# A low-rank update on one core: sixteen tokens a partition in each part, and two more engines' programs as loops

## The chip, the cores and the metric

The kernel runs on one core of one Trainium2 chip. The metric is device time in microseconds of one execution; the time before is the median of three runs. "Span" is the time between the first and the last instruction of one execution that was recorded by the hardware profiler. Engines are named as in the profile: PE is TensorE, DVE is VectorE, ACT is ScalarE, POOL is GpSimd and SP is SyncE.

## What is computed

```python
def setup_inputs():
    batch, seq, d_model, r = 16, 512, 768, 16
    # x [16, 512, 768], A [768, 16], B [16, 768], float32; scale 0.5

def reference(x, A, B, scale):
    lora = np.matmul(np.matmul(x, A), B)
    return (x + scale * lora).astype(np.float32)
```

There are 8192 tokens of 768 numbers. Each token is read once (25.2 MB), gets a rank-16 correction and is written once (25.2 MB).

## The kernel before

**Layout.** The 8192 tokens are 64 "token slots" of 128 partitions each; all of x stays on the chip in one tile, xs, of 64 slots x 768 float32 a partition. SyncE issues the transfers: eight loads of 2, 2, 4, 8, 8, 8, 16 and 16 slots, and ten stores of 2, 2, 4 and then 8 slots each (lists LOADS and STORES). Within a load of n slots a partition holds n consecutive tokens, so that its row is one contiguous run of n x 3 KB. All go through one queue, in the order of issue: loads 0 and 1, A, B, the other loads, then the stores. The last load goes over the place where A and B stood in float32, so SyncE waits for their conversion (prep) before it. Each store waits for a count of the semaphore added.

**Chunks.** Work goes by chunks of four slots, 16 in all. For each chunk:

- the four slots are narrowed to float16 in three tiles of 256 columns: xh0 and xh1 by VectorE, xh2 by ScalarE (function narrowed, L92 and L94). Each tile has one buffer;
- TensorE transposes them in six groups of four 128x128 matmuls with an identity (turned(0) to turned(5), L186), into three PSUM buffers; turned(0) and turned(1) read xh0, turned(2) and turned(3) xh1;
- ScalarE moves each group to the float16 tiles xt (L136);
- TensorE projects with A in six steps (projected(0) to projected(5), L194); ScalarE scales the result to yt (L140);
- TensorE multiplies with B, slot by slot (expanded(0) to expanded(3), L205), into two PSUM buffers lo_ps; VectorE adds each to xs in place (summed, L147) and posts freed.

**Order.** The engines are not tied by a scheduler; each has a program written out by hand, and semaphores between them. TensorE's program is a hardware loop over chunks; it consumes its semaphores one at a time (taken: wait for at least 1, then take 1 away). One pass is:

```python
for j in range(NX):            # NX = 3
    turned(j)
first()                        # both(0): expanded(0), expanded(1) of the chunk before
for j in range(NX, ND):        # ND = 6
    projected(j - NX)
    turned(j)
second()                       # both(2): expanded(2), expanded(3) of the chunk before
for j in range(NX, ND):
    projected(j)
```

Every expanded takes one freed, so that it waits for the sum two slots earlier. VectorE's and ScalarE's programs are written out for all 16 chunks and wait for absolute counts. VectorE does, in chunk c: refill xh0 for chunk c + 1 as soon as turned has counted turned(1) of chunk c, two sums of chunk c - 1, refill xh1 after turned(3), two more sums. A drain follows the last sum of each store, and posts added.

**Start.** VectorE narrows chunk 0, transposes A (L159), converts it to a_mm (L163) and B to b_mm (L165), and posts prep; TensorE's first projection waits for that.

Of the kernel before, what the change touches and what calls it, by code (L numbers as in the profile page):

```python
# [9 lines left out]
MM_DT = mybir.dt.float16  # L10


LOADS = [2, 2, 4, 8, 8, 8, 16, 16]
STORES = [2, 2, 4, 8, 8, 8, 8, 8, 8, 8]

CHUNK = 4

# [2 lines left out]
def kernel(  # L20
# [8 lines left out]
    nc = tc.nc  # L29
    fp32 = mybir.dt.float32  # L30
    add = mybir.AluOpType.add
    P = 128

    x2 = x.flatten_outer_dims()
    out2 = out.flatten_outer_dims()
    T, D = x2.shape
    R = A.shape[1]
    NT = T // P
    NC = NT // CHUNK
    ND = D // P  # L40
    NU = ND // 2
    NX = 3
    W = 2 * P
    NB = D // 32
# [4 lines left out]
    sb = ctx.enter_context(tc.tile_pool(name="sb", bufs=1))  # L49
    ps = ctx.enter_context(tc.tile_pool(name="ps", bufs=1, space=bass.MemoryType.PSUM))  # L50

    xs = sb.tile([P, NT, D], fp32, name="xs")
    ident = sb.tile([P, P], MM_DT, name="ident")
    a_mm = sb.tile([P, ND, R], MM_DT, name="a_mm")
    b_mm = sb.tile([R, D], MM_DT, name="b_mm")
    xh = [sb.tile([P, CHUNK, W], MM_DT, name=f"xh{u}") for u in range(NU)]
    xt = [sb.tile([P, CHUNK * P], MM_DT, name=f"xt{j}") for j in range(ND)]
    yt = sb.tile([R, CHUNK * P], MM_DT, name="yt")
    xt_ps = [ps.tile([P, CHUNK * P], fp32, name=f"xt_ps{b}") for b in range(NX)]
    yt_ps = ps.tile([R, CHUNK * P], fp32, name="yt_ps")  # L60
    lo_ps = [ps.tile([P, D], fp32, name=f"lo_ps{b}") for b in range(2)]
# [5 lines left out]
    b_f32 = xs[0:R, room + 2, :]  # L67

    def rows(t2, t0, n):
        return t2[ds(t0 * P, n * P), :].rearrange("(p s) d -> p s d", s=n)  # L70

    with tc.tile_critical():  # L72
        names = "zeroed ident a b a_t prep fed0 fed1 fed2 turned got proj y lora freed added".split()
        S = {k: nc.alloc_semaphore(name=f"s_{k}") for k in names}
        landed = [nc.alloc_semaphore(name=f"s_load{i}") for i in range(len(LOADS))]
        stored = nc.alloc_semaphore(name="s_stored")
        part_of = [i for i, n in enumerate(LOADS) for _ in range(n)]

        def load(i):
            t0, n = sum(LOADS[:i]), LOADS[i]  # L80
            nc.sync.dma_start(out=xs[:, t0 : t0 + n, :], in_=rows(x2, t0, n)).then_inc(landed[i], 16)

        known = set()

        def narrowed(engine, c, u):
            for i in sorted({part_of[c * CHUNK + s] for s in range(CHUNK)}):
                if (engine.engine, i) not in known:
                    known.add((engine.engine, i))
                    engine.wait_ge(landed[i], 16)
            src = xs[:, ds(c * CHUNK, CHUNK), ds(u * W, W)]  # L90
            if engine is nc.scalar:
                i = engine.copy(out=xh[u], in_=src)  # L92
            else:
                i = engine.tensor_copy(out=xh[u], in_=src)  # L94
            i.then_inc(S[f"fed{u}"], 1)


        nc.gpsimd.memset(a_rows, 0.0).then_inc(S["zeroed"], 1)  # L98
        nc.gpsimd.memset(ident, 0.0).then_inc(S["zeroed"], 1)  # L99
        nc.gpsimd.wait_ge(S["zeroed"], 2)  # L100
        nc.gpsimd.affine_select(  # L101
            out=ident, in_=ident, compare_op=mybir.AluOpType.not_equal, fill=1.0,
            base=0, pattern=[[-1, P]], channel_multiplier=1,
        ).then_inc(S["ident"], 1)


        load(0)
        load(1)
        nc.sync.wait_ge(S["zeroed"], 1)
        nc.sync.dma_start(  # L110
            out=a_rows[0:NB, :, :], in_=A.rearrange("(b a) r -> b a r", a=32)
        ).then_inc(S["a"], 16)
        nc.sync.dma_start(out=b_f32, in_=B).then_inc(S["b"], 16)
        for i in range(2, len(LOADS) - 1):
            load(i)
        nc.sync.wait_ge(S["prep"], 1)
        load(len(LOADS) - 1)
        done = 0
        for k, n in enumerate(STORES):
            i = part_of[done]  # L120
            t0, w = sum(LOADS[:i]), LOADS[i]
            nc.sync.wait_ge(S["added"], k + 1)
            piece = slice(done - t0, done - t0 + n)
            nc.sync.dma_start(
                out=rows(out2, t0, w)[:, piece, :], in_=xs[:, done : done + n, :]
            ).then_inc(stored, 16)
            done += n

        nc.gpsimd.wait_ge(stored, 16 * len(STORES))


        narrowed(nc.scalar, 0, 2)
        for c in range(NC):
            for j in range(ND):
                nc.scalar.wait_ge(S["turned"], ND * c + j + 1)
                nc.scalar.copy(out=xt[j], in_=xt_ps[j % NX]).then_inc(S["got"], 1)  # L136
            if c + 1 < NC:
                narrowed(nc.scalar, c + 1, 2)
            nc.scalar.wait_ge(S["proj"], c + 1)
            nc.scalar.activation(  # L140
                out=yt, in_=yt_ps, func=mybir.ActivationFunctionType.Copy, scale=sc
            ).then_inc(S["y"], 1)


        def summed(k):
            nc.vector.wait_ge(S["lora"], k + 1)
            nc.vector.tensor_tensor(  # L147
                out=xs[:, k, :], in0=xs[:, k, :], in1=lo_ps[k % 2], op=add
            ).then_inc(S["freed"], 1)
            if k + 1 in ends:  # L150
                nc.vector.drain().then_inc(S["added"], 1)  # L151

        ends = {sum(STORES[: i + 1]) for i in range(len(STORES))}
        nc.vector.sem_inc(S["freed"], 2)
        narrowed(nc.vector, 0, 0)
        narrowed(nc.vector, 0, 1)

        nc.vector.wait_ge(S["a"], 16)
        nc.vector.transpose(out=a_t, in_=a_rows.rearrange("b a r -> b r a")).then_inc(S["a_t"], 1)  # L159
        nc.vector.wait_ge(S["a_t"], 1)  # L160
        a_tv = a_t[:, :, 0:NB].rearrange("a r (c k) -> a k c r", k=4)
        for k in range(4):
            nc.vector.tensor_copy(out=a_mm[ds(32 * k, 32), :, :], in_=a_tv[:, k, :, :])  # L163
        nc.vector.wait_ge(S["b"], 16)
        nc.vector.tensor_copy(out=b_mm, in_=b_f32).then_inc(S["prep"], 1)  # L165
        for c in range(NC):
            for u in range(2):
                if c + 1 < NC:
                    nc.vector.wait_ge(S["turned"], ND * c + 2 * u + 2)
                    narrowed(nc.vector, c + 1, u)  # L170
                if c >= 1:
                    for s in range(2 * u, 2 * u + 2):
                        summed((c - 1) * CHUNK + s)
        for s in range(CHUNK):
            summed((NC - 1) * CHUNK + s)


        def taken(name):
            nc.tensor.wait_ge(S[name], 1).then_inc(S[name], -1)  # L179

        def turned(j):
            u, h = divmod(j, 2)
            if h == 0:
                taken(f"fed{u}")
            for s in range(CHUNK):
                i = nc.tensor.matmul(  # L186
                    xt_ps[j % NX][:, ds(s * P, P)], xh[u][:, s, ds(h * P, P)], ident,
                    start=True, stop=True,
                )
            i.then_inc(S["turned"], 1)  # L190

        def projected(j):
            taken("got")
            i = nc.tensor.matmul(  # L194
                yt_ps, a_mm[:, j, :], xt[j], start=(j == 0), stop=(j == ND - 1)
            )
            if j == ND - 1:
                i.then_inc(S["proj"], 1)

        def expanded(s):  # L200
            if s == 0:
                taken("y")
            taken("freed")
            for n0, w in n_splits:
                i = nc.tensor.matmul(  # L205
                    lo_ps[s % 2][:, ds(n0, w)], yt[:, ds(s * P, P)], b_mm[:, ds(n0, w)],
                    start=True, stop=True,
                )
            i.then_inc(S["lora"], 1)

        def chunk(first, second):
            for j in range(NX):
                turned(j)
            first()
# [3 lines that stand above are left out]
            second()  # L218
            for j in range(NX, ND):
                projected(j)  # L220

        def both(s):
            expanded(s)
            expanded(s + 1)

        nc.tensor.wait_ge(S["ident"], 1)
        chunk(lambda: nc.tensor.wait_ge(S["prep"], 1), lambda: None)
        with nc.Fori(1, NC, engines=(mybir.EngineType.PE,)):
            chunk(lambda: both(0), lambda: both(2))
        for s in range(CHUNK):  # L230
            expanded(s)
# [35 lines left out]
```

## Time and profile before

| | |
|---|---|
| median of three runs | 125.25 us (125.25 to 125.34) |
| the profiled execution | 125.31 us, span 123.5 us |
| busy: PE, DVE, ACT | 84.3, 80.2, 76.2 us |
| bytes, mean rate over the span | 50.45 MB, 408 GB/s |
| share of the span in which the queue's packets fill the 16 DMA engines | 96.4% |
| last sum of VectorE done, last store issued, last store landed | 101.1, 101.2, 122.5 us |

The page's second part cuts the span into 40 slices of 3.1 us; a digit is the busy share in tenths. A timeline line gives start, duration, engine, line, operation, output and inputs, how many in a row, and in brackets the idle time before it with what ended that. A line of windows gives a stretch, its length, the busy time of PE, PEld, DVE, ACT and POOL with numbers of instructions, the granted TensorE clock, the share of the DMA engines and GB/s.

### The profile page before, as it was taken

To read this page: it belongs to the slowest core of one execution; us is meant where nothing else is said; L and a number is where in the kernel's file an instruction comes from. 1 tells how busy PE (TensorE), PEld (TensorE's weight loads), DVE (VectorE), ACT (ScalarE), POOL (GpSimd) and SP (SyncE) were. 2 spreads that over 40 slices of the span, in tenths; PEclk is the share of its full clock that TensorE was granted. 3 is DMA by queue.
4 is the path that set the end of the run, shared out by engine and by line. 5 is a ranking of instruction groups with operands and counts; after the bars stand their busy time and mean duration, and the time that the engine had idled before them with its cause. 6 is when DMAs were issued, how large, how long until landed. Compare 5 with 4: busy or idle time off the path is not lost. (4 is left out here: it accounts for less than half of the span.)

```text
span 123.5 us, 1804 instructions
## 1 busy us (share of the span) xinstructions
PE 84.3 (68%) x608; PEld 39.7 (32%) x608; DVE 80.2 (65%) x102; ACT 76.2 (62%) x129; POOL 1.1 (1%) x7
## 2 busy tenths in 40 slices
PE   0024986999999999999999999999999420000000
PEld 0022342444445444454444544445444100000000
DVE  0049208888999999999899999999977770000000
ACT  0047598469889898898988989889896100000000
POOL 3000000000000000000000000000000000000000
PEclk9999999589999999999999999999999975555555
DMA  3999999999999699899889999999999999999990
GB/s 86 414 396 426 477 398 454 422 406 469 414 509 477 302 496 493 382 401 477 288 366 448 434 477 398 446 438 398 477 398 446 438 398 485 390 454 438 390 414 16
DMA packets 2662, 50.45 MB, mean 408 GB/s; under 512 B 316, under 2 KB 316, under 8 KB 868
## 3 DMA queue, kind: packets, MB, share of 16 engines
q1 hardware_dynamic: 2660, 50.43, 96.4%
q14 instruction: 2, 0.02, 0.0%
HBM read 25.26 MB, written 25.17 MB: 408 GB/s over the span
## 5 line engine op out<-in xcount | busy, mean ns | idle before, releaser
L147 DVE TENSOR_TENSOR xs<-xs,lo_ps 128x768 f32<-128x768 f32 x64 | 58.1, 950 | 5.5 <-PE lo_ps L205 4.8
L136 ACT CAST xt<-xt_ps 128x512 f16<-128x512 f32 x96 | 52.4, 577 | 10.1 <-PE xt_ps L186 8.4
L186 PE MATMUL xt_ps<-ident,xh 128*128 128x128 f16 x384 | 34.4, 229 | 8.6 <-PEq L179 8.6
L194 PE MATMUL yt_ps<-xt,a_mm 128*16 128x512 f16 x96 | 32.9, 396 | 1.8 <-PEq L179 1.6
L94 DVE CAST xh<-xs 128x1024 f16<-128x1024 f32 x32 | 22.0, 689 | 15.3 <-DMA xs<-in_x_dram 13.1
L186 PEld LDWEIGHTS xt_ps<-ident,xh 128*128 128x128 f16 x384 | 23.0, 102 | 26.9 <-issue 26.9
L205 PE MATMUL lo_ps<-b_mm,yt 16*128 16x512 f16 (+1 forms) x128 | 26.6, 324 | 5.4 <-PEq L179 3.5
L92 ACT CAST xh<-xs 128x1024 f16<-128x1024 f32 x16 | 16.8, 1048 | 0.0
L205 PEld LDWEIGHTS lo_ps<-b_mm,yt 16*128 16x128 f16 x128 | 9.6, 92 | 15.2 <-issue 9.5
L194 PEld LDWEIGHTS yt_ps<-xt,a_mm 128*16 128x16 f16 x96 | 7.1, 87 | 17.8 <-issue 13.0
L140 ACT ACTIVATE yt<-yt_ps 16x512 f16<-16x512 f32 x16 | 9.4, 587 | 2.6 <-PE yt_ps L194 2.6
L92 ACT ACT_TABLE_LOAD x1 | 1.3, 1283 | 7.8 <-DMA xs<-in_x_dram 7.8
L159 DVE STREAM_TRANSPOSE xs<-xs 32x512 f32<-32x512 f32 x1 | 1.0, 1037 | 0.0
L163 DVE CAST a_mm<-xs 32x96 f16<-32x96 f32 x4 | 0.9, 231 | 0.1
L165 DVE CAST b_mm<-xs 16x768 f16<-16x768 f32 x1 | 0.5, 548 | 0.0
L98 POOL MEMSET xs<- 32x512 f32 x1 | 0.5, 514 | 0.5 <-SPq L72 0.5
L101 POOL TENSOR_SCALAR_AFFINE_SELECT ident<-ident 128x128 f16<-128x128 f16 x1 | 0.3, 292 | 0.2 <-POOL ident L99 0.2
L99 POOL MEMSET ident<- 128x128 f16 x1 | 0.2, 194 | 0.0
L248 POOL MEMSET const-bfloat16-1.0<- 128x1 bf16 x1 | 0.1, 101 | 0.0
L248 POOL MEMSET const-uint8-127<- 128x1 uint8 x1 | 0.1, 101 | 0.0
L248 POOL MEMSET const-float32-0.0<- 128x1 f32 x1 | 0.1, 98 | 0.2 <-issue 0.2
L248 POOL MEMSET const-float32-1.0<- 128x1 f32 x1 | 0.1, 98 | 0.0
## 6 DMA issues: line engine op xcount, KB each, us to landing
out_dram<-xs SPq DMA_DIRECT2D x7, 3072.0 KB, 29.4
xs<-in_x_dram SPq DMA_DIRECT2D x2, 6144.0 KB, 48.0
xs<-in_x_dram SPq DMA_DIRECT2D x3, 3072.0 KB, 22.3
xs<-in_x_dram SPq DMA_DIRECT2D x2, 768.0 KB, 5.3
xs<-in_x_dram SPq DMA_DIRECT2D x1, 1536.0 KB, 8.8
out_dram<-xs SPq DMA_DIRECT2D x2, 768.0 KB, 44.2
out_dram<-xs SPq DMA_DIRECT2D x1, 1536.0 KB, 41.5
xs<-in_A_dram SPq DMA_DIRECT2D x1, 48.0 KB
```

What stands on the lines that cost most here:

```text
L92: i = engine.copy(out=xh[u], in_=src)
L94: i = engine.tensor_copy(out=xh[u], in_=src)
L98: nc.gpsimd.memset(a_rows, 0.0).then_inc(S["zeroed"], 1)
L136: nc.scalar.copy(out=xt[j], in_=xt_ps[j % NX]).then_inc(S["got"], 1)
L140: nc.scalar.activation(out=yt, in_=yt_ps, func=mybir.ActivationFunctionType.Copy, scale=sc).then_inc(S["y"], 1)
L147: nc.vector.tensor_tensor(out=xs[:, k, :], in0=xs[:, k, :], in1=lo_ps[k % 2], op=add).then_inc(S["freed"], 1)
L159: nc.vector.transpose(out=a_t, in_=a_rows.rearrange("b a r -> b r a")).then_inc(S["a_t"], 1)
L163: nc.vector.tensor_copy(out=a_mm[ds(32 * k, 32), :, :], in_=a_tv[:, k, :, :])
L165: nc.vector.tensor_copy(out=b_mm, in_=b_f32).then_inc(S["prep"], 1)
L186: i = nc.tensor.matmul(xt_ps[j % NX][:, ds(s * P, P)], xh[u][:, s, ds(h * P, P)], ident, start=True, stop=True,)
L194: i = nc.tensor.matmul(yt_ps, a_mm[:, j, :], xt[j], start=(j == 0), stop=(j == ND - 1))
L205: i = nc.tensor.matmul(lo_ps[s % 2][:, ds(n0, w)], yt[:, ds(s * P, P)], b_mm[:, ds(n0, w)], start=True, stop=True,)
```

## The change

Tokens are laid out anew: each part of 16 slots gives a partition 16 consecutive tokens. There are six loads (2, 6 and 8 slots of the first part, then 16, 16, 16) and four stores of 16 slots. VectorE's and ScalarE's programs become hardware loops, with taken as in TensorE's. Slots of xs are addressed by the loop's register. GpSimd waits for the loads and passes them on, one okv (to VectorE) and one oka (to ScalarE) a chunk. The refills of xh0 and xh1 wait for new semaphores, read0 and read1, which projected(0) and projected(2) post. ScalarE converts A to a_mm and first touches a column of the identity; GpSimd converts B to b_mm (prepb).

```diff
-LOADS = [2, 2, 4, 8, 8, 8, 16, 16]
-STORES = [2, 2, 4, 8, 8, 8, 8, 8, 8, 8]
+PART = 16
+LOADS = [2, 6, 8, 16, 16, 16]
+STORES = [16, 16, 16, 16]
...
     def rows(t2, t0, n):
-        return t2[ds(t0 * P, n * P), :].rearrange("(p s) d -> p s d", s=n)
+        part = t2[ds(t0 // PART * PART * P, PART * P), :].rearrange("(p s) d -> p s d", s=PART)
+        return part[:, ds(t0 % PART, n), :]
...
+        def taken(engine, name):
+            engine.wait_ge(S[name], 1).then_inc(S[name], -1)
...
+            nc.sync.wait_ge(S["added"], (done + n) // CHUNK)
...
+        for c in range(NC):
+            for i in sorted({part_of[c * CHUNK + k] for k in range(CHUNK)}):
+                if part_of.index(i) >= c * CHUNK:
+                    nc.gpsimd.wait_ge(landed[i], 16)
+            nc.gpsimd.sem_inc(S["okv"], 1)
+            nc.gpsimd.sem_inc(S["oka"], 1)
+            if c == 0:
+                nc.gpsimd.wait_ge(S["b"], 16)
+                nc.gpsimd.tensor_copy(out=b_mm, in_=b_f32).then_inc(S["prepb"], 1)
...
+        nc.scalar.wait_ge(S["ident"], 1)
+        nc.scalar.copy(out=first, in_=ident[:, 0:1])
+        taken(nc.scalar, "oka")
+        narrowed(nc.scalar, 0, 2)
+        nc.scalar.wait_ge(S["a_t"], 1)
+        a_tv = a_t[:, :, 0:NB].rearrange("a r (c k) -> a k c r", k=4)
+        for k in range(4):
+            i = nc.scalar.copy(out=a_mm[ds(32 * k, 32), :, :], in_=a_tv[:, k, :, :])
+        i.then_inc(S["prep"], 1)
+        with nc.Fori(CHUNK, NT - CHUNK + 1, CHUNK, engines=(mybir.EngineType.Activation,)) as t:
+            evicted()
+            taken(nc.scalar, "oka")
+            narrowed(nc.scalar, t, 2)
+            scaled()
+        evicted()
+        scaled()
...
+        def refilled(t, u):
+            taken(nc.vector, f"read{u}")
+            if u == 0:
+                taken(nc.vector, "okv")
+            narrowed(nc.vector, t, u)
...
-        for c in range(NC):
-            for u in range(2):
-                if c + 1 < NC:
-                    nc.vector.wait_ge(S["turned"], ND * c + 2 * u + 2)
-                    narrowed(nc.vector, c + 1, u)
-                if c >= 1:
-                    for s in range(2 * u, 2 * u + 2):
-                        summed((c - 1) * CHUNK + s)
+        refilled(CHUNK, 0)
+        refilled(CHUNK, 1)
+        with nc.Fori(0, NT - 3 * CHUNK + 1, CHUNK, engines=(mybir.EngineType.DVE,)) as t:
+            refilled(t + 2 * CHUNK, 0)
+            summed(t, (0, 1))
+            refilled(t + 2 * CHUNK, 1)
+            summed(t, (2, 3))
+            nc.vector.drain().then_inc(S["added"], 1)
+        for t in (NT - 2 * CHUNK, NT - CHUNK):
+            summed(t, range(CHUNK))
+            nc.vector.drain().then_inc(S["added"], 1)
...
         def projected(j):
-            taken("got")
+            taken(nc.tensor, "got")
             i = nc.tensor.matmul(
                 yt_ps, a_mm[:, j, :], xt[j], start=(j == 0), stop=(j == ND - 1)
             )
+            if j in (0, 2):
+                i.then_inc(S[f"read{j // 2}"], 1)
```

VectorE's loop makes 14 passes and ScalarE's 15; TensorE's order of work stays as it was.

## Prediction

> **What bounds the kernel now.** First the page: how full the queue of transfers is, slice by slice (a slice is 3.1 us; the last sum ends in the 33rd).
>
> ```profile
> DMA  3999999999999699899889999999999999999990
> GB/s 86 414 396 426 477 398 454 422 406 469 414 509 477 302 496 493 382 401 477 288 366 448 434 477 398 446 438 398 477 398 446 438 398 485 390 454 438 390 414 16
> ...
> q1 hardware_dynamic: 2660, 50.43, 96.4%
> ```
>
> Transfers fill the span from end to end: the kernel is bound by its 50.4 MB. SyncE issues all loads first, so stores queue behind them. The answer on the tensor out_dram shows how deep that queue still is at the end, and the timeline when the last sum and the last store come:
>
> ```profile
> L124 SPq DMA_DIRECT2D out_dram<-xs x10: 332/332/348, 21.4 to 101.2; - x10
> ...
> DMA to landing us min/median/max: 21.3/33.9/44.5
> ```
>
> ```profile
> 97.55 3.55 DVE L147 TENSOR_TENSOR xs<-xs,lo_ps 128x768 f32<-128x768 f32 x4 [0.65 <-PE lo_ps L205]
> ```
>
> The last sums run to 101.1, the last store is issued at 101.2 and lands 21.3 later, at 122.5, though its 3.15 MB need only 7.3 us (the four windows from 100 to 120 us give 467, 398, 467 and 398, mean 432 GB/s). So compute has 14 us of slack against the queue. The question is how much of it the change spends. Compute's own rhythm comes from the windows over a steady chunk and from its timeline:
>
> ```profile
> 50.72:55.86 5.14, 5.00 (x38) 2.38 (x39) 4.97 (x7) 4.66 (x9) 0.00 (x0) 1.00 0.90 384
> ```
>
> ```profile
> 50.78 0.69 DVE L94 CAST xh<-xs 128x1024 f16<-128x1024 f32 x1 [0.20 <-PE xt_ps L186]
> ...
> 54.88 0.84 PE L186 MATMUL xt_ps<-ident,xh 128*128 128x128 f16 x12
> ...
> 55.65 0.69 DVE L94 CAST xh<-xs 128x1024 f16<-128x1024 f32 x1
> ...
> 55.83 0.45 PEld L205 LDWEIGHTS lo_ps<-b_mm,yt 16*128 16x128 f16 x4 [0.29 <-issue]
> 56.38 1.82 DVE L147 TENSOR_TENSOR xs<-xs,lo_ps 128x768 f32<-128x768 f32 x2
> 56.60 0.38 PE L194 MATMUL yt_ps<-xt,a_mm 128*16 128x512 f16 x1
> ```
>
> A chunk takes 5.14 us, and in it TensorE is busy 5.00, VectorE 4.97, ScalarE 4.66. VectorE starts the next chunk's cast (55.65) while TensorE is still in the transposes, before it expands (55.83) and projects (56.60).
>
> **The change: VectorE's refill waits for more.** Before, refilled slot 0 waits for the count of turned(1): the transposes that read xh0. After, it waits for read0, which projected(0) posts. In TensorE's unchanged order projected(0) stands behind both(0), and expanded(1) in there waits for freed of the previous chunk's last sum. That closes a ring: sum 3, expanded(1), projected(0), refill of xh0, sums 0 and 1, refill of xh1, sums 2 and 3. Before, the refill filled just that gap. Behind the waiting refill VectorE's sums are queued in order, and for them wait TensorE (freed) and the stores (added). The gap can be read where TensorE already waits for a sum, early in the timeline:
>
> ```profile
> 19.51 1.81 DVE L147 TENSOR_TENSOR xs<-xs,lo_ps 128x768 f32<-128x768 f32 x2
> ...
> 21.44 0.12 PEld L205 LDWEIGHTS lo_ps<-b_mm,yt 16*128 16x128 f16 x2 [0.74 <-issue]
> ...
> 21.88 0.10 PEld L194 LDWEIGHTS yt_ps<-xt,a_mm 128*16 128x16 f16 x2 [0.32 <-issue]
> ```
>
> The sum ends at 19.51 + 1.81 = 21.32; the weights freed by it load at 21.44 (0.12); the projection follows at 21.88 (0.44) and takes 0.38 at full clock. Together 0.94 us. Then VectorE: two counted takes (read0, okv) and an instruction that works out the address from the loop's register. A take costs about 0.14 at TensorE: from ScalarE's yt (54.98 + 0.59 = 55.57) to the weights at 55.83, with two takes, 0.26, against 0.12 with one. Bounds for this term: 0.06 and 0.7 (five takes); I take 0.3, near two. The drain, the register add and the branch at the end of each pass lie under the 0.94 and cost nothing; uncovered they would cost about 0.3 a pass. The rest of the ring is the old run from refill to last sum, 50.78 to 53.91 + 1.82 = 55.73, so 4.95. New period: 4.95 + 0.94 + 0.3 = 6.2 us instead of 5.14. A second ring is as long and hides nothing: sum 1 ends 1.24 + 2.4 after sum 3; then 0.12, 0.44, three projections 0.81, yt 0.59 and 0.3, and 0.4 for expanded(0), 6.3 to expanded(1).
>
> **Loops.** The instruction streams shrink; TensorE's own loop shows what a back edge costs: from its last projections to the next pass's transposes 54.13 + 0.81 = 54.94 against 54.87, nothing. [...] The sum goes by the row.
>
> **Start.** Chunk 0 now waits for 8 slots instead of 4: 1.57 MB more at 432 GB/s, 3.64 us. GpSimd relays the landing with a semaphore, 0.15 (one take; bounds 0.05 and 0.3). The casts start at 7.78 + 3.8 = 11.6. A follows load 1 as before and lands under the casts. Then two casts 1.21 and the transposition 1.04; a_mm, now on ScalarE, 4 x 0.231 by VectorE's row, or 4 x 0.19 by the line through ScalarE's 577 ns for 512 and 1048 ns for 1024 elements; and an eviction of 0.58, now queued behind them. That is 3.75 where before had 3.91 (7.78 to 11.69), so the shift stays about 3.8. b_mm on GpSimd has no row: 0.55 on VectorE is the nearest, and it could take 2 us under the projections without a waiter. Before, chunk 1's first projection began at 18.02; with 0.38, the shift 3.8 and the 0.3 it releases the loop's first refill at 22.5. The slots it needs, within the first 16, landed by 18.9, as before. Slots 16 to 31 land near 33 (12.6 MB at 432 from 2 us, and 2 more) and are wanted at 34.9.
>
> **End.** The loop's fourteenth pass starts at 22.5 + 13 x 6.2 = 103.1, its last sum ends at 108.05. Chunks 14 and 15 have no refills: before they ran from 92.41 (the sums' start in the timeline) to 101.11, 8.7; with 0.3 for drain and branch the last sum is done at 117.05. The last store is now 6.29 MB and finds the queue empty (the third is issued near 96 and done by 112): 14.55 us of data, and 2.6 around them (load 0, into an empty queue, lands 4.4 after its issue, of which 0.79 MB take 1.8). Issue 0.07, after landing 1.0 (122.5 to 123.5). Span 117.05 + 0.07 + 17.15 + 1.0 = 135.2. The profiled execution took 125.31 for a span of 123.5, 1.8 more (the median is 125.25): **137.0 us**. In short, time = 56.4 + 13 x period; the old span comes back at a period of 5.30, so only 0.16 of slack a chunk is left once the last store has doubled and the start is 3.8 later.
>
> **Rivals.** *The queue stays the bound* (not slower): if projected(0) comes before VectorE needs it, or the period stays below 5.30, time is set by bytes. From 2 to 120.5 us they ran at 426 GB/s; at 432 throughout, with fewer and larger packets, they would need up to 1.9 us less: 123.4 to 125.3, at 124.6. For it: 96.4% and the 14 us. Against: VectorE is busy 4.97 of 5.14. Chance 0.06. *Only the takes cost*: the wait for read0 is covered and the separate takes add 0.3 to 0.55 a chunk: 127.3 to 130.5, at 129. Chance 0.12. *The forecast*: gap 0.94 and 0.06 to 0.7: 134 to 142. Chance 0.62. *TensorE's clock falls too*:
>
> ```profile
> 18.60:21.90 3.30, 2.33 (x18) 0.89 (x16) 2.87 (x4) 2.70 (x4) 0.00 (x0) 1.00 1.07 462
> 22.00:25.30 3.30, 3.30 (x18) 1.69 (x17) 2.57 (x4) 1.99 (x4) 0.00 (x0) 0.50 1.01 432
> ...
> 93.70:97.00 3.30, 2.42 (x16) 0.90 (x14) 2.34 (x3) 2.02 (x4) 0.00 (x0) 1.00 1.07 462
> ```
>
> After a stretch with TensorE busy 2.33 of 3.30 the granted clock was 0.50; after 2.42 it stayed 1.00 for the next stretch. With 5.00 of 6.2 (81%) on average, single stretches can fall to the 2.33 of 3.30 (71%). The three groups from 21.88 on then took 1.40, 1.46 and 1.19 instead of 0.81, 0.84 and 0.81: 1.6 us. Every second chunk so, the period is 7.0: 147, with 142 to 150 around it. Chance 0.20. [...]
>
> **Numbers.** Half of each neighbour is inside 129 to 145. A measurement tells 0.2% from no change. Faster 0.05 and same 0.01 share the first rival; slower 0.94.
>
> **What would show it.** Right: stores' last issue near 117, slices with DMA below 9 before the last two stores, VectorE idle about 1.2 us a chunk before L94, put down to PE yt_ps. Wrong start: first casts not near 11.6. Wrong ring: 14 passes not 6.2 apart; a period under 5.3 ends it. Granted clock of 0.50 mid-loop speaks for the last rival.

## The result and the profile after

The changed kernel took 144.3 to 149.4 us in six runs (median 147.46); its faster runs stand to those of the kernel before as 1.153, interval 1.1507 to 1.1553. The times go with the granted TensorE clock: 0.864 at 144.26 us, 0.806 at 149.4. The profiled execution is one of 147.33 us with a span of 145.3 us and a mean clock of 0.832, so it shows more of what halves the clock than the fastest run does. The forecast was 137.0, range 129 to 145; the two faster runs (144.26 and 144.55) lie just inside the range, in the place of the last rival, and the other four lie above it.

The page's slices (3.6 us each now) and queue:

```profile
PEclk9999999999999965995999985555589999955555
DMA  4998999999999999999999997000099990059995
GB/s 120 431 450 386 480 447 433 433 419 447 433 433 419 433 447 419 406 433 447 433 433 433 433 433 338 0 0 0 0 433 433 433 433 0 0 216 433 433 433 217
...
q1 hardware_dynamic: 1508, 50.43, 81.4%
```

The queue runs dry twice, before the third and before the fourth store, and the clock row has 5s in the middle of the loop, which before stood only at 22 to 25 us and behind the last chunk. The tensor out_dram:

```profile
L122 SPq DMA_DIRECT2D out_dram<-xs x4: 332/338/348, 47.3 to 128.4; - x4
...
DMA to landing us min/median/max: 15.9/17.2/30.5
```

The last store is issued at 128.4 and lands 15.9 us later: its own bytes and nothing before it. The ring of a chunk at full clock, from the timeline of all engines:

```profile
26.52 1.81 DVE L172 TENSOR_TENSOR xs<-xs,lo_ps 128x768 f32 x2
...
27.50 0.59 ACT L146 ACTIVATE yt<-yt_ps 16x512 f16<-16x512 f32 x1 [1.01 <-ACTq L87]
...
28.35 0.45 PEld L228 LDWEIGHTS lo_ps<-b_mm,yt 16*128 16x128 f16 x4 [0.38 <-issue]
...
29.11 0.38 PE L215 MATMUL yt_ps<-xt,a_mm 128*16 128x512 f16 x1
...
29.86 0.69 DVE L94 CAST xh<-xs 128x1024 f16 x1 [1.53 <-DVEq L87]
```

The last sum ends at 28.33, both(0) loads its weights from 28.35, the projection runs from 29.11 to 29.49, and only then, at 29.86, VectorE refills xh0. It has waited 1.53 us. The profile puts this down to VectorE's sequencer at L87, the line of taken: a take is recorded there as an instruction of its own. From VectorE's timeline later on, a refill after a stretch at half clock and one after a chunk at full clock:

```profile
70.37 0.69 DVE L94 CAST xh<-xs 128x1024 f16 x1 [2.77 <-DVEq L87]
...
76.65 0.69 DVE L94 CAST xh<-xs 128x1024 f16 x1 [1.53 <-DVEq L87]
```

Refill to refill at full clock is 6.28 us (70.37 to 76.65). Of the thirteen distances between the loop's fourteen refills five are 7.5 to 8.75 instead; together they are 8.8 us over five times 6.28. What stands before such a stretch is in the windows (PE busy is the second number, the granted clock the one before the DMA share):

```profile
45.20:48.60 3.40, 3.17 (x26) 1.48 (x24) 1.98 (x3) 2.14 (x5) 0.00 (x0) 1.00 0.97 419
48.60:52.00 3.40, 2.56 (x18) 1.05 (x17) 3.29 (x5) 2.70 (x4) 0.00 (x0) 1.00 1.07 463
52.00:55.40 3.40, 3.40 (x19) 1.61 (x16) 1.46 (x2) 2.10 (x4) 0.00 (x0) 0.50 1.07 463
55.40:58.80 3.40, 3.40 (x18) 1.30 (x16) 2.25 (x3) 1.17 (x2) 0.00 (x0) 0.50 1.07 463
62.20:65.60 3.40, 2.56 (x18) 1.09 (x18) 2.75 (x4) 2.84 (x5) 0.00 (x0) 1.00 0.97 419
65.70:69.10 3.40, 3.40 (x18) 1.56 (x17) 1.90 (x3) 1.62 (x5) 0.00 (x0) 0.51 0.94 405
75.90:79.30 3.40, 2.56 (x19) 1.17 (x19) 2.65 (x4) 2.84 (x5) 0.00 (x0) 1.00 1.08 463
82.70:86.10 3.40, 2.56 (x19) 0.99 (x17) 3.17 (x5) 2.70 (x4) 0.00 (x0) 1.00 1.07 463
86.20:89.50 3.30, 3.30 (x18) 1.68 (x17) 1.49 (x2) 2.10 (x4) 0.00 (x0) 0.50 1.10 477
```

After the stretch from 48.6, with TensorE busy 2.56 of 3.40 (75%), the clock fell to 0.50, and likewise after those from 62.2 and from 82.7 (2.56 each). After the one from 75.9, also 2.56, it did not, nor after those from 24.7, 41.8 and 113.4 (2.57, 2.56 and 2.56). It fell after three of seven such stretches, all at 75%; what tells the three from the four is not shown. The trace has the clock change at 51.99, 58.81, 65.64, 69.05, 86.12 and 106.60 us, each time a whole multiple of 3.41 us after the change before, and the stretches above are cut to these steps.

### The profile page after: what moved, and what is told of

Same layout as the page of the kernel before. It is cut to its first block, busy times and chain, and to the rows that moved or that the text cites. A ratio compares the mean times of both kernels' runs of the same rounds, so it can differ in the third digit from the quotient of the medians.

```text
span 145.3 us, 2254 instructions
## 1 busy us (share of the span) xinstructions
PE 98.6 (68%) x608; PEld 43.1 (30%) x608; DVE 78.2 (54%) x97; ACT 78.8 (54%) x134; POOL 2.0 (1%) x8
## 5 line engine op out<-in xcount | busy, mean ns | idle before, releaser
L142 ACT CAST xt<-xt_ps 128x512 f16<-128x512 f32 x96 | 52.6, 581 | 17.1 <-ACTq L87 15.7
L172 DVE TENSOR_TENSOR xs<-xs,lo_ps 128x768 f32 (+1 forms) x64 | 57.9, 948 | 2.9 <-DVEq L87 2.9
L94 DVE CAST xh<-xs 128x1024 f16 (+1 forms) x32 | 22.6, 710 | 47.2 <-DVEq L87 45.7
L207 PE MATMUL xt_ps<-ident,xh 128*128 128x128 f16 x384 | 39.0, 249 | 12.4 <-PEq L87 12.4
L228 PE MATMUL lo_ps<-b_mm,yt 16*128 16x512 f16 (+1 forms) x128 | 31.5, 355 | 13.7 <-PEq L87 11.5
L215 PE MATMUL yt_ps<-xt,a_mm 128*16 128x512 f16 x96 | 37.4, 448 | 2.4 <-PEq L87 2.4
L207 PEld LDWEIGHTS xt_ps<-ident,xh 128*128 128x128 f16 x384 | 26.2, 110 | 34.6 <-issue 34.6
L92 ACT CAST xh<-xs 128x1024 f16 (+1 forms) x16 | 16.8, 1048 | 9.0 <-ACTq L87 9.0
L215 PEld LDWEIGHTS yt_ps<-xt,a_mm 128*16 128x16 f16 x96 | 7.3, 89 | 21.3 <-issue 17.3
L157 ACT CAST a_mm<-xs 32x96 f16<-32x96 f32 x4 | 1.4, 349 | 1.8 <-DVE xs L188 1.8
L135 POOL CAST b_mm<-xs 16x768 f16<-16x768 f32 x1 | 0.8, 830 | 9.7 <-DMA xs<-in_B_dram 9.7
```

The costliest lines, as they stand in the source:

```text
L135: nc.gpsimd.tensor_copy(out=b_mm, in_=b_f32).then_inc(S["prepb"], 1)
L157: i = nc.scalar.copy(out=a_mm[ds(32 * k, 32), :, :], in_=a_tv[:, k, :, :])
L172: nc.vector.tensor_tensor(out=xk, in0=xk, in1=lo_ps[k % 2], op=add).then_inc(S["freed"], 1)
L207: i = nc.tensor.matmul(xt_ps[j % NX][:, ds(s * P, P)], xh[u][:, s, ds(h * P, P)], ident, start=True, stop=True,)
L215: i = nc.tensor.matmul(yt_ps, a_mm[:, j, :], xt[j], start=(j == 0), stop=(j == ND - 1))
L228: i = nc.tensor.matmul(lo_ps[s % 2][:, ds(n0, w)], yt[:, ds(s * P, P)], b_mm[:, ds(n0, w)], start=True, stop=True,)
```

## The experiments

Periods below are from refill to refill of xh0 at full clock, where nothing else is said; times are medians, beside 125.25 to 125.28 of the kernel before.

**e1, the refill's release moved.** The one edit:

```diff
 def turned(j):
...
+                if s == 0 and j in (2, 4):
+                    i.then_inc(S[f"read{j // 2 - 1}"], 1)
...
 def projected(j):
-            if j in (0, 2):
-                i.then_inc(S[f"read{j // 2}"], 1)
```

> read0 and read1 are posted by the first matmul of turned(2) and of turned(4) instead of by projected(0) and projected(2); all else is as in the changed kernel. Theory (the ring through the projection sets the period, 6.28 us at full clock, and the idle time it gives TensorE is what halves the clock): period back to 5.2 to 5.5, granted clock 1.00 all through the loop, last store issued by about 105, time 125 to 128. Rival (loops and counted takes are slow by themselves): period stays above 6, time above 138. Second rival (the doubled last store and the late start alone are the loss): time stays above 138 with a short period.

Measured: 128.63 us (128.54 to 128.69), ratio 1.027 (1.0246 to 1.0286). VectorE's timeline:

```profile
50.88 0.69 DVE L94 CAST xh<-xs 128x1024 f16 x1 [0.80 <-DVEq L87]
...
56.44 0.69 DVE L94 CAST xh<-xs 128x1024 f16 x1 [0.80 <-DVEq L87]
```

The period is 5.55 (the time and the period are both just above the theory's ranges), and the clock never falls in the loop (1.00 from 50.88 to 56.44, mean of the run 0.926): 16 to 21 us of the loss hang on which matmul posts the release. The rest is a period 0.4 longer than the 5.14 of before. The last sum ends at 109.74, the last store is issued at 109.8 (5 us above my expectation of 105) and lands 15.9 later. The sum of the prediction, 56.4 + 13 x period, gives 128.6.

**e2, the wait alone.** The kernel before with this edit:

```diff
-                    nc.vector.wait_ge(S["turned"], ND * c + 2 * u + 2)
+                    nc.vector.wait_ge(S[f"read{u}"], c + 1)
```

and read0, read1 posted by projected(0) and projected(2).

> The kernel before, written out and with its loads and stores, in which VectorE's refills of xh0 and xh1 wait for counts posted by projected(0) and projected(2). Theory: the ring alone makes the period 5.9 to 6.1 at full clock (gap 0.94 to 1.2, no takes on VectorE and ScalarE), some stretches at half clock, last sum at 113 to 122 instead of 101, a last store of 3.15 MB (7.3 and 2.6) behind it: 126 to 135. Rivals: the wait costs nothing in a program without loops, 125.3.

Measured: 125.45 us, ratio 1.0012 (0.9992 to 1.0031): no difference, as the rival had it, but for another reason. VectorE's timeline and the tensor out_dram:

```profile
54.15 0.69 DVE L94 CAST xh<-xs 128x1024 f16<-128x1024 f32 x1 [1.11 <-PE yt_ps L194]
...
60.01 0.69 DVE L94 CAST xh<-xs 128x1024 f16<-128x1024 f32 x1 [1.11 <-PE yt_ps L194]
```

```profile
DMA to landing us min/median/max: 13.1/30.0/43.7
```

The wait is there, 1.11 us a chunk, with the name I had expected it under, and the period is 5.86. The last sum ends at 109.3 instead of 101.1. But the last store is issued into a queue that still needs 13.1 us (before: 21.3), and lands at 122.5 as before. The ring took 8.2 of the 14 us of slack and nothing else. I had put the last sum at 113 to 122, because I counted on stretches at half clock; TensorE stayed busy 2.81 to 3.26 of 3.40 us in four windows (2.75 in the emptiest of the loop), and its clock stayed at 1.00.

**e3, TensorE kept busy.** The changed kernel, with matmuls of zeros where TensorE waits:

```diff
+        def filled(n):
+            for _ in range(n):
+                nc.tensor.matmul(
+                    yt_bank[64:128, 0:256], ident[:, 0:64], nought, start=True, stop=True
+                )
...
         def both(s):
+            filled(2 if s == 0 else 3)
             expanded(s)
+            if s == 2:
+                filled(3)
             expanded(s + 1)
```

> The changed kernel with idle matmuls in TensorE's loop: two of 256 columns before expanded(0), three each before expanded(2) and expanded(3), into partitions 64 to 127 of the projection's PSUM bank, from a tile of zeros; they lie where TensorE waited 0.23, 0.45 and 0.39 us. Theory (what lies above about 138 is the halved clock, and the clock follows how full TensorE's stretches are): granted clock 1.00 through the loop, period 6.3 to 6.5, time 137.5 to 141, runs within 1 us of each other. Rival (the long periods have another cause, or idle matmuls do not count): 144 to 150 as in the changed kernel, runs spread over 5 us.

Measured: 140.81 us (140.77 to 141.06). More work makes the kernel 3.5 to 8.6 us faster than the changed one. Its page and a window over one chunk:

```profile
PEclk9999999999999999999999999999999999955555
```

```profile
49.29:55.62 6.33, 6.32 (x47) 2.95 (x46) 4.75 (x6) 4.71 (x8) 0.00 (x0) 1.00 0.88 380
```

TensorE is busy throughout, the granted clock holds, all 13 periods of the loop are 6.34 and the runs lie within 0.3 us. So the spread of the changed kernel and all of it above about 140 is the halved clock.

**e4 and e7, small last stores.** e4 is the changed kernel, e7 is e3, each with `STORES = [16, 16, 16, 4, 4, 4, 4]`.

> The changed kernel with stores of 16, 16, 16 and then 4, 4, 4, 4 slots. Theory (after the last sum only the last store's own bytes are left, 6.29 MB or 14.6 us in the changed kernel, 1.57 MB or 3.6 us here): 10.9 us less than the changed kernel, 133 to 138 with the same spread from the clock. Rival (stores wait behind each other anyway): no gain over 3 us.

e4: 142.42 us (139.51 to 144.26), about 5 less than the changed kernel, between the two expectations. The profiled run, the slowest, had seven long periods instead of five (mean clock 0.796, not 0.832), so the clock hid part of the gain; hence e7.

> e3 (idle matmuls that keep the clock at 1.00, period 6.34) with stores of 16, 16, 16, 4, 4, 4, 4. Theory (behind the last sum only the last store's own bytes are left; e4 gained less than 9 us only because its runs had more stretches at half clock): last sum at 121.6 as in e3, landing 6.4 after it instead of 15.9, 131.0 to 131.8. Rival (small stores themselves lengthen the loop): last sum later than 122.5, 133 or more.

e7: 132.92 us (132.84 to 133.64), 7.9 less than e3 at the same period (6.34). The last sum ends at 121.5, as in e3; the last store lands 8.1 us after its issue, not 6.4: the store before it, issued 5 us earlier, is not yet through. The last store's size was worth 7.9 us, a little less than I had expected.

**e5, e11 and e10, the transfers without loops.** e5 is the kernel before with the new layout, loads and stores.

> The kernel before, programs written out, with the changed kernel's six loads and four stores of 16 slots a partition. Theory (a longer period is what makes the doubled last store and the late start count): period stays 5.14, last sum near 104.5 because the start is 3.4 to 3.8 later, last store lands 15.9 later near 120.5: the queue and the last sum end nearly together, 123.5 to 125.3. Rival (the transfers' new sizes cost several us by themselves): 127 or more.

Measured: 127.0 to 135.5 us in six runs. That is the rival's time, but neither expectation foresaw the cause or the spread. VectorE's timeline and the windows of the same stretch in the profiled run (127.18):

```profile
33.56 0.69 DVE L96 CAST xh<-xs 128x1024 f16<-128x1024 f32 x1 [2.45 <-DMA xs<-in_x_dram]
```

```profile
29.00:33.50 4.50, 4.36 (x34) 2.04 (x32) 1.85 (x3) 4.08 (x8) 0.00 (x0) 1.00 1.14 492
33.50:38.00 4.50, 2.83 (x20) 1.38 (x20) 4.44 (x6) 2.59 (x5) 0.00 (x0) 0.93 0.88 382
38.00:42.00 4.00, 4.00 (x21) 1.70 (x18) 3.41 (x5) 2.02 (x4) 0.00 (x0) 0.50 1.14 492
42.00:47.00 5.00, 5.00 (x24) 2.12 (x23) 1.82 (x2) 3.04 (x5) 0.00 (x0) 0.50 0.86 374
```

With a period of 5.14 the fifth chunk wants its slots 2.45 us before the first load of 16 lands; TensorE runs out of work (2.83 of 4.50), and some 10 us at half clock follow. The last store is issued at 108.4. Of the other runs there is no timeline; their granted clocks go with their times (0.880 at 127.02 us, 0.812 at 135.48). In the changed kernel the same load is wanted later and delays nobody (refill at 36.15, no longer wait than in other chunks). e11 splits that load: `LOADS = [2, 6, 8, 8, 8, 16, 16]`.

> e5 with one edit: the fourth load of 16 slots split in two of 8. Theory (the spread of e5 comes from the fifth chunk waiting 2.45 us for that load): no such wait, granted clock 1.00 from there, last sum 104 to 106, last store of 16 slots lands 15.9 later, 123.8 to 125.8 with little spread. Rival (the spread comes from the late start or from the stores): 127 to 135 as in e5.

e11: 125.28 us, ratio 1.0001 (0.9989 to 1.0013), twelve runs within 0.5. No wait for data in the loop, the last sum at 102.6 (I had expected 104 to 106), and the last store lands 19.9 later. So the late start and the four stores of 16 slots cost nothing at the old period. e10 keeps the new layout with loads of 2, 2, 4, 8, 8, 8, 16, 16 and stores of 16, 16, 16, 8, 8.

> The kernel before, written out, with the layout of 16 slots a part, its own loads 2, 2, 4, 8, 8, 8, 16, 16 and stores of 16, 16, 16, 8, 8 instead of ten. Theory: period 5.14, last sum 101, the queue full to its end: the bytes set the time, 124.4 to 125.4, and larger packets are worth at most 0.8. Rival (the layout or large stores cost the queue): 125.6 or more.

e10: 125.31 us, ratio 1.0006 (0.9988 to 1.0025). The theory's range, but at its end: larger and fewer packets are worth nothing that can be measured.

**e8, e6 and e9, the loops.** e8 is e1 with ScalarE's program written out and waiting for absolute counts.

> e1 with ScalarE's program written out again, waiting for absolute counts instead of taking; VectorE's loop stays. If the 0.40 us a chunk that e1 has over the kernel before comes from takes on ScalarE's path (transposes, eviction, projection, yt): period 5.15 to 5.3, time 124.5 to 125.5. If it comes from VectorE's loop (takes, address instructions, drain and branch): period stays 5.5, time 128 to 129.

e8: 128.18 us, period 5.55. The 0.4 a chunk is not ScalarE's. VectorE's loop makes it, by e1's own trace: its casts and sums take 4.75 us of a chunk and the gap 0.80, together the whole period. The gap holds VectorE's own instructions end to end: 0.43 from the last sum's end (50.08) through drain, register add, branch and register move, and 0.37 for two takes and the address. The take of read0 at 50.56 waits for nothing, since read0 was posted at 49.74. e6 and e9 look for a version of the loops that is as fast as before: e1 with shorter first loads and last stores, e6 with `LOADS = [2, 2, 4, 8, 16, 16, 16]`, e9 with `[2, 2, 4, 8, 8, 8, 16, 16]`.

> Loops, takes and read0/read1 posted by the transposes as in e1, with loads of 2, 2, 4, 8, 16, 16, 16 and stores of 16, 16, 16, 8, 8. Theory: period 5.55 as in e1, start as before the change, last sum near 106, so that the queue is never empty before the last store and the bytes bound the kernel again: 124.0 to 125.2, at or a little below the kernel before. Rival (loops cost the queue something too, or large packets run slower): 126 or more.

e6: 126.1 to 133.6 us (median 127.72), again a wait for the first load of 16 (the refill at 33.59 had waited 3.92) and a mean clock of 0.870 in that run of 128.73 us; the slowest had 0.831.

> As e6 (loops, read0/read1 posted by the transposes, stores of 16, 16, 16, 8, 8), with the loads 2, 2, 4, 8, 8, 8, 16, 16 of the kernel before. Theory (in e5 and e6 the first load of 16 slots lands 2.5 to 4 us after the fifth chunk wants it, and that idle time halves TensorE's clock): no refill waits for data after 20 us, granted clock 1.00 from 26 us on, period 5.55, last sum 105 to 107, 124.2 to 125.4, runs within 0.5 us. Rival (loops halve the clock by their own idle time): 126 to 133 with the spread of e6.

e9: 126.17 us (126.06 to 126.29), ratio 1.007 (1.0052 to 1.0088). The wait and the spread are gone, period 5.55, last sum at 105.95, and the last store lands 17.1 later, so it had others before it. That is 0.8 us more than I expected at most. The span ends 0.7 later than before (124.2), and 2.0 instead of 1.8 lie outside it; why, is open. No version beat the kernel before.

## Why the prediction came out as it did

*The ring* held. It was named before the run, e1 undoes it, and its period was 6.28 against 6.2. What sets the period is the second ring of the prediction (6.3), through sum 1, the projections and yt. expanded(0) starts 0.26 after yt ends (28.09 to 28.35), as in the kernel before (55.57 to 55.83); in e2 it even starts before the last sum ends (52.97 against 53.04). The first ring, through the last sum (28.33), is almost as long. The gap was mis-sized, 1.53 against 1.24: 0.76 for both(0) stand where I had 0.12 and 0.44, and 0.36 for takes and address instead of 0.3. The sums ran a little closer together than in the chunk I had taken (4.75 instead of 4.95), which made up for most of it.

*"Lie under the 0.94 and cost nothing"* held too: in the trace VectorE's drain, add, branch and register move are over at 28.79, and the projection that it then waits for ends at 29.49. The loops lengthen the ring by other instructions. From e2 (5.86, written out) to the changed kernel (6.28) it grows by 0.42, and 0.32 of that lie between the projection's end and the refill, the two takes and the address (0.36 against 0.04). Uncovered, as in e1, drain, add, branch and register move take 0.43; my 0.3 a pass was an estimate with no row of before behind it.

*The start* came out 1.1 late (first refill of the loop at 23.58, not 22.5), though the casts were early (11.31, not 11.6). Two rows of the timeline hold most of it:

```profile
11.31 1.92 DVE L94 CAST xh<-xs 128x1024 f16<-128x1024 f32 x2 [11.31 <-DVEq L87]
```

```profile
14.21 1.43 ACT L157 CAST a_mm<-xs 32x96 f16<-32x96 f32 x4 [1.80 <-DVE xs L188]
```

VectorE's two casts took 1.92 instead of 1.29, and a_mm on ScalarE 1.43: 0.35 each, above both rows by which I had bounded it.

*The end* was nearly as summed: 9.5 from the fourteenth pass's last sum (118.81) to the last (128.28), where I had 9.0, and 15.9 instead of 17.15 to the landing.

*The step that failed* is the place of the clock. At full clock the sum is nearly right: 147.33 less the 8.8 us of long periods is 138.5, against 137.0. The late start (1.1) and thirteen periods 0.08 longer (1.0) are in part made up by the landing (1.25 less). e3, which keeps the clock at the price of a period 0.06 longer, took 140.8. But I gave the halved clock 0.20, and the rival's price (142 to 150) was the result. That the two faster runs lie inside the range is luck: it reached to 145 to take in half of that rival, and the forecast's own end was 142. I had read the row, 71% halves, and set it against an average of 81% in the new period. TensorE's busy time in a chunk is not even: it waits for the sums in one half, and single stretches fell to 75%, after which the clock fell three times and held four times. No long pause stands before these falls: the longest time without a matmul in the loop is 0.45 us.

*Rivals.* That only the takes cost is what e1 measures, 128.6 at my 129, but without the wait. The queue as the bound is e2's result: the ring alone is free. So the loss is no sum of parts. The ring (e2: +0.2), the transfers (e11, one load split: 0) and the loops with short ends (e9: +0.9) cost next to nothing each; a longer period costs 13 times itself only once the late start and the doubled last store have used up the slack, and then the clock comes on top. Two small sums of the rivals are off, without consequence: at 432 GB/s the bytes need 1.8 us less, not 1.9, and 0.3 to 0.55 a chunk gives 127.1 to 130.4 by the formula.

## What to carry to other kernels

Post the release of a buffer as soon as the last instruction that reads it is through (e1 posts from the matmul behind it), not from a later one that is convenient: the difference is which queue of waits stands between (e1: 128.63 us, the changed kernel 144.3 to 149.4). Slack in the queue hid a longer loop (e2: period 5.86, 125.45 us) until the last transfer was made larger (e1: 5.55, with a later start too, 128.63), so judge such changes together, by the time from the last result to the landing of the last transfer. And where a loop leaves TensorE idle for part of each pass, look at the emptiest 3.4 us of it and not at its mean before counting on the full clock: here TensorE was busy 5.21 of 6.28 on average and 2.56 of 3.40 in the emptiest stretches, and after three of seven of these the clock was 0.50.

## What was not expected of the hardware

Work without use made the kernel faster: 120 idle matmuls (608 became 728) took 147.5 to 140.8 us by holding the clock (mean 0.935 in the profiled run, 0.832 without them). A single wait of 2.45 us early in e5's profiled run was followed by some 10 us at half clock; its six runs took 2 to 10 us more than the kernel before, and e11, without the wait, took 125.28. While GpSimd cast b_mm (11.85 to 12.68), VectorE's second cast took 1.31 instead of 0.69 us (from 11.92). It is so in all eight traces in which GpSimd makes that cast (1.92 for VectorE's two casts), and in none of the five in which VectorE makes it (1.29 or 1.30); no run tests it by itself.
